# A two-layer encoder trunk: the order of every engine's instructions taken from the scheduler's other machine model

## The chip, the cores and the metric

The kernel runs on one core of a Trainium2 chip. A core has five engines that each work through an instruction list of their own, in the order in which it was written: TensorE (in the profile PE, its weight loads PEld), VectorE (DVE), ScalarE (ACT), GpSimd (POOL) and SyncE (SP), which here issues nearly all DMA transfers. They meet only at semaphores: an instruction that has to wait for another engine holds up everything behind it on its own list.

The metric is the device time of one execution in microseconds (us). Lower is better.

## The reference

One sequence of 1024 tokens of width 1024 goes through two layers. Layer 0 mixes tokens with multi-head latent attention (8 heads, a low-rank query and key/value, a rotary part, a mask by chunks of 64). Layer 1 mixes them with an mLSTM, a matrix memory that is carried from chunk to chunk. After each follows a gated MLP of width 2816 with a causal width-3 convolution. Every sub-layer is normalised, and shifted, scaled and gated by a vector that is computed from the conditioning `c`.

```python
for i in range(2):
    mod = silu(c) @ mod_w[i] + mod_b[i]
    sh_a, sc_a, g_a, sh_f, sc_f, g_f = split(mod, 6)
    h = rms_norm(x) * (1 + sc_a) + sh_a
    y = mla_mixer(h, ...) if i == 0 else mlstm_mixer(h, ...)
    x = x + g_a * y
    h = rms_norm(x) * (1 + sc_f) + sh_f
    a, g = split(h @ w_up, 2)
    a = causal_conv3(a, conv_w, conv_b)
    x = x + g_f * ((gelu(a) * g) @ w_down)
return rms_norm(x, final_norm)
```

All inputs and outputs are float32.

## The kernel before

**Precision and units of work.** Every float32 operand of a large matrix product is split into a rounded part (`whi`, `h` and so on, written by ACT) and the rest (`wlo`, written by DVE or POOL). One product of two tiles is then three TensorE instructions, the lines 175, 176 and 177 of the function `mm3`; each streams 512 columns as a rule. A weight tile comes by a DMA on SP's queue (`wraw`, `raw`, `mraw`), ACT casts it (line 167 or 988), DVE subtracts (168 or 989), and TensorE uses it.

**Stages.** They follow each other in the program text with some overlap: the input projection of both token halves (tiles `ia`); the attention, 16 turns of one head and one token half, in which the score blocks (`sc`, line 673), the turning of the weights (`pT`, 696), the product with the values (`pv`) and the projections of the next head (`qp`, `kp`, `qrp`, `vp`) are woven into each other by a written list of steps; the output projection (`op`); the MLP, in which each 2x2 block of products is done with 7 instead of 8 products, first the upward part (`pa`, `pb`, `pd`), then the downward part (`da`, `db`), whose operands `U` are rebuilt on ACT and DVE from `u` read back from DRAM; the mLSTM, whose matrix `C` is a serial chain of 7 links for each of 4 heads (lines 1471 to 1476) and is covered by projections (`inp`) placed between the links; and again an output projection and an MLP. The conditioning is not a matrix product: a row of 1024 numbers is multiplied and summed on DVE in one instruction (`mod_dot`, line 198), 96 of these rows in all, spread over the stages.

**What sets the order.** The function `trunk_kernel` is traced once, as plain Python; each call appends an instruction. The tile framework notes what depends on what. When the `with` block closes, its scheduler runs the program on a model of the machine. Whenever an engine of the model is free, it gets that instruction among those whose inputs and buffers are ready in the model which has the highest priority. Priority is the place in the program text, raised inside `tc.high_priority()`. `tc.keep_in_program_order` ties an instruction behind the one that was traced before it on its engine. The order that comes out is fixed for each engine, the semaphore waits are put in afterwards, and on the chip each engine follows its list whatever the real durations are. So the model has a say wherever it takes an instruction for not yet ready: what is behind it in the text then goes ahead of it.

How far that goes can be counted in the built program, the scheduled list of each engine against the traced one. Of TensorE's 10,421 matrix instructions 89% stand at their place in the text, and in both MLPs' upward parts nearly all. On DVE 11% do, and one is moved by 6.5 places on average; on ACT 16% and 3.6 places; on SP's queue of 746 transfers 14% and 7.3 places.

**Lookahead.** In the MLPs the weights of a product are made several products before it is run (`LOOK = (7, 5)`: for the first products the product and the seven behind it, later the product and the five behind it); they lie in four buffers of two halves each (`open_weights(4, 2)`), and raw tiles in `RAWS = 5`. In the attention two turned tiles are made ahead (`TURN = 2`). PSUM has four `mm` tiles, and four of another kind that depends on the stage.

The two places of the code that the steps of the prediction come back to are the chain of the mLSTM and the row product:

```python
with tc.high_priority():
    dve.scalar_tensor_tensor(Cn, C, gcl(GDEC, hd, cc), pc, ALU.mult, ALU.add)   # 1473 (1471 at the first link)
    C = Cn
    act.activation(Cs[0], C, AF.Copy)                                           # 1475
    dve.tensor_tensor(Cs[1], C, Cs[0].bitcast(F32), ALU.subtract)               # 1476
...
tc.keep_in_program_order(mod_dot(l, j * 8 + k, raw, c))                         # 198, in mod_steps
```

The function that the change touches:

## Time and profile before

| | |
|---|---|
| Median of 3 runs | 2197.2 us (2195.38 to 2199.59) |
| Span of the profiled execution | 2200.1 us; no other time is given for it |
| TensorE busy | 2166.5 us, 98% of the span |
| TensorE weight loads (beside the matmuls) | 1818.0 us, 83% |
| VectorE busy | 1693.1 us, 77% |
| ScalarE busy | 1046.7 us, 48% |
| GpSimd busy | 178.3 us, 8% |
| Mean granted TensorE clock | 0.994 of full speed |
| DMA | 270.50 MB, mean 123 GB/s |

Busy time is the share of the span in which the engine had an instruction in work. TensorE's instructions overlap: each is recorded with a duration of some 0.39 us while one starts every 0.23 us, so the share says how seldom TensorE stood still, not how fast it went. The profiled execution lies 2.9 us above the median of the runs; a difference that is worked out in the trace is therefore taken over to the median as it is.

### The profile page before, as it was taken

Reading aid. Unit: us, or ns where it says so; the run is one execution under the profiler, and the core shown is the slowest. Engines: PE = TensorE matmul, PEld = TensorE weight load, DVE = VectorE, ACT = ScalarE, POOL = GpSimd, SP = SyncE. Lnnn points to the kernel's source line nnn. Section 1 sums busy time; section 2 is a strip of 40 time slices with the busy share of each in tenths; the row PEclk is TensorE's granted clock in tenths of the full one; section 3 lists DMA queues with packets and bytes.
Section 4 is the critical chain, followed back from the end, with each engine's and each line's share of the span. In section 5 each row is a group of like instructions: output and inputs, shape, how many; then the busy total and the mean of one; then the engine's idle time right before and its main releaser. Section 6 shows DMA issues by size and latency. Waiting matters only on the chain.

```text
span 2200.1 us, 28740 instructions
## 1 busy us (share of the span) xinstructions
PE 2166.5 (98%) x10557; PEld 1818.0 (83%) x10557; DVE 1693.1 (77%) x2769; ACT 1046.7 (48%) x1812; POOL 178.3 (8%) x216
## 2 busy tenths in 40 slices
PE   9999999999999999999999999999999999999998
PEld 7878888787888888877888888988788888887787
DVE  8877878669878777899973655566887777778997
ACT  6465556446544444543453434344554444453335
POOL 0000000000000000042210111010000000002232
PEclk9999999999999999999999999999999999999999
DMA  8512234832444332542132243444143332245122
GB/s 317 152 50 63 92 109 142 285 125 69 157 139 143 123 125 85 204 151 89 53 121 93 62 131 103 132 157 171 64 144 101 111 120 92 79 163 194 50 80 77
DMA packets 105085, 270.50 MB, mean 123 GB/s; under 512 B 12336, under 2 KB 15984, under 8 KB 104944
## 3 DMA queue, kind: packets, MB, share of 16 engines
q1 hardware_dynamic: 104544, 268.28, 36.9%
q8 instruction: 83, 1.36, 0.3%
q14 instruction: 58, 0.48, 0.1%
q10 hardware_dynamic: 400, 0.39, 0.1%
HBM read 221.53 MB, written 44.47 MB: 121 GB/s over the span
## 4 chain that ended last, share of the span: by engine, by line
PE 85%; DVE 9%; DMA 3%; ACT 2%; issue 1%; POOL 0%; SPq 0%; POOLq 0%; DVEq 0%; ACTq 0%
PE pa L175 7%; PE pa L177 7%; PE pa L176 7%; PE pd L177 3%; PE pd L175 3%; PE pd L176 3%; PE sc L673 3%; PE op L175 3%; PE op L176 3%; PE op L177 2%; PE inp L177 2%; PE da L175 2%; PE inp L175 2%; PE inp L176 2%; PE da L176 2%; PE db L175 2%
## 5 line engine op out<-in xcount | busy, mean ns | idle before, releaser
L988 ACT ACTIVATE whi<-raw 128x512 fp32r<-128x512 f32 (+1 forms) x252 | 147.3, 607 | 243.2 <-PE pb L176 61.0
L988 ACT ACTIVATE whi<-wsum 128x512 fp32r<-128x512 f32 (+1 forms) x224 | 134.0, 617 | 181.8 <-PE pa L176 61.5
L175 PE MATMUL pa<-T,whi 128*128 128x512 f32 x528 | 205.9, 390 | 0.0
L176 PE MATMUL pa<-T,whi 128*128 128x512 f32 x528 | 205.4, 389 | 0.0
L177 PE MATMUL pa<-T,wlo 128*128 128x512 f32 x528 | 205.1, 389 | 0.0
L989 DVE TENSOR_TENSOR wlo<-wsum,whi 128x512 fp32r<-128x512 f32 (+1 forms) x224 | 151.1, 690 | 32.8 <-ACT whi L988 31.5
L989 POOL TENSOR_TENSOR wlo<-raw,whi 128x512 fp32r<-128x512 f32 (+1 forms) x80 | 119.9, 1515 | 401.7 <-ACT whi L988 394.0
L175 PE MATMUL da<-U,whi 128*128 128x512 f32 (+1 forms) x364 | 139.5, 383 | 3.4 <-DVE x L294 3.4
L177 PE MATMUL da<-U,wlo 128*128 128x512 f32 (+1 forms) x364 | 138.4, 383 | 2.0 <-DVE wlo L989 2.0
L176 PE MATMUL da<-U,whi 128*128 128x512 f32 (+1 forms) x364 | 139.2, 382 | 0.0
L989 DVE TENSOR_TENSOR wlo<-raw,whi 128x512 fp32r<-128x512 f32 (+1 forms) x172 | 115.7, 679 | 24.9 <-ACT whi L988 24.9
L167 ACT ACTIVATE whi<-wraw 128x1024 fp32r<-128x1024 f32 x67 | 70.7, 1059 | 117.1 <-PE op L176 59.2
L175 PEld LDWEIGHTS pa<-T,whi 128*128 128x128 f32 x528 | 99.1, 188 | 22.2 <-ACT whi L988 1.2
L177 PEld LDWEIGHTS pa<-T,wlo 128*128 128x128 f32 x528 | 99.1, 188 | 20.6
L176 PEld LDWEIGHTS pa<-T,whi 128*128 128x128 f32 x528 | 99.1, 188 | 20.3
L1140 DVE TENSOR_TENSOR U<-q,U 128x1024 fp32r<-128x1024 f32 x84 | 102.9, 1241 | 14.0 <-ACT U L1139 13.6
L1028 ACT ACTIVATE ct<-a,cols 128x512 f32<-128x512 f32 x88 | 70.8, 808 | 83.9 <-DVE a L1050 47.9
L175 PE MATMUL db<-U,whi 128*128 128x512 f32 x264 | 103.3, 391 | 1.3 <-ACT whi L988 1.3
L168 DVE TENSOR_TENSOR wlo<-wraw,whi 128x1024 fp32r<-128x1024 f32 x67 | 81.7, 1222 | 29.4 <-ACT whi L167 27.2
L177 PE MATMUL db<-U,wlo 128*128 128x512 f32 x264 | 102.9, 390 | 0.0
L176 PE MATMUL db<-U,whi 128*128 128x512 f32 x264 | 102.8, 389 | 0.0
L1139 ACT ACTIVATE U<-q 128x1024 fp32r<-128x1024 f32 x84 | 79.7, 979 | 47.7 <-DVE q L1138 22.2
(378 smaller groups left out, 6097.3 us busy)
## 6 DMA issues: line engine op xcount, KB each, us to landing
raw<-in_wf SPq DMA_DIRECT2D x96, 512.0 KB, 4.0
wraw<-in_w SPq DMA_DIRECT2D x67, 512.0 KB, 3.7
mraw<-in_mod_w SPq DMA_DIRECT2D x56, 512.0 KB, 4.0
ud<-ct SPq DMA_DIRECT2D x88, 256.0 KB, 2.4
q<-ud SPq DMA_DIRECT2D x88, 256.0 KB, 4.6
raw<-in_wd SPq DMA_DIRECT2D x32, 512.0 KB, 6.4
pa<-in_mod_w SPq DMA_DIRECT2D x24, 512.0 KB, 3.7
x<-xd SPq DMA_DIRECT2D x48, 256.0 KB, 4.8
```

The lines of the kernel that those rows point to most:

```text
L167: act.activation(hi, raw, AF.Copy)
L168: dve.tensor_tensor(lo, raw, hi.bitcast(F32), ALU.subtract)
L175: pe.matmul(ps, lh, rh, start=first, stop=False, skip_group_check=more)
L176: pe.matmul(ps[:, 0:rl.shape[-1]], lh, rl, start=False, stop=False, skip_group_check=more)
L177: pe.matmul(ps, ll, rh, start=False, stop=last, skip_group_check=more)
L673: pe.matmul(ps[:, cs], a[:, qs if n < 3 else qrs_], b[:, cs], start=n == 0, stop=n == 4)
L988: act.activation(hi, src, AF.Copy)
L989: eng.tensor_tensor(lo, src, hi.bitcast(F32), ALU.subtract)
L1028: act.activation(t, a[:, 2:], AF.Identity, bias=col(f"cb{l}", m), scale=cw(m, 2))
L1139: act.activation(hi, w, AF.Copy)
L1140: dve.tensor_tensor(lo, w, hi.bitcast(F32), ALU.subtract)
```

## The change

The flag `schedule_with_timeline_sim` of the tile framework is set. The scheduler then runs the program on its other machine model (a simulator of timelines, in which each instruction holds devices for stretches of time) instead of the default one. The traced program, its dependencies, its priorities, the tiles, their buffers and the computation are the same; the order on each engine, and with it the places of the semaphore waits, is what the scheduler makes of the other model's times.

```diff
-    with tile.TileContext(nc) as tc:
+    with tile.TileContext(nc, schedule_with_timeline_sim=True) as tc:
         trunk_kernel(tc, *args)
```

## The prediction

> **What bounds the kernel now.** I read the page's busy shares and the clock first, then the busy time by stages, then who TensorE waited for, and last the order of the instructions around single waits.
>
> ```profile
> span 2200.1 us, 28740 instructions
> PE 2166.5 (98%) x10557; PEld 1818.0 (83%) x10557; DVE 1693.1 (77%) x2769; ACT 1046.7 (48%) x1812; POOL 178.3 (8%) x216
> ...
> core 0: 2200.1 us, clock 0.994
> ```
>
> TensorE stood still for 2200.1 - 2166.5 = 33.6 us. The mean clock of 0.994 is 0.006 x 2200.1 = 13 us of lost full speed more. The same 10,557 matmuls run in any order, so an order can win at most 33.6 + 13 = 47 us; it can lose without a bound that this page shows. Where the 33.6 us lie is told by the windows (length, then busy time and number of instructions of PE, PEld, DVE, ACT and POOL, clock, DMA):
>
> ```profile
> 0.00:110.00 110.00, 105.22 (x504) 87.99 (x505) 91.57 (x162) 57.51 (x89) 7.63 (x14) 0.97 0.68 234
> 110.00:400.00 290.00, 284.14 (x1585) 243.88 (x1583) 228.18 (x488) 171.91 (x352) 5.50 (x30) 0.99 0.32 99
> ...
> 535.00:930.00 395.00, 395.00 (x1743) 326.40 (x1742) 318.65 (x508) 183.13 (x299) 1.79 (x18) 1.00 0.43 143
> 930.00:1110.00 180.00, 177.01 (x777) 145.14 (x776) 166.71 (x210) 72.41 (x115) 58.65 (x40) 1.00 0.28 95
> 1110.00:1500.00 390.00, 384.99 (x2256) 337.51 (x2255) 227.11 (x470) 165.33 (x332) 34.95 (x40) 1.00 0.38 123
> ...
> 1595.00:1990.00 395.00, 395.00 (x1742) 326.42 (x1741) 302.41 (x474) 182.84 (x299) 1.79 (x18) 1.00 0.37 122
> 1990.00:2145.00 155.00, 151.30 (x662) 123.42 (x661) 145.30 (x184) 59.07 (x90) 46.91 (x28) 1.00 0.28 92
> 2145.00:2200.10 55.10, 46.53 (x257) 40.14 (x255) 40.68 (x65) 31.03 (x65) 16.37 (x15) 0.92 0.22 77
> ```
>
> The two upward parts of the MLPs, 790 us, have no idle time at all and full clock: 395.00 / 1743 = 0.2266 us from one matmul to the next. The idle time is 4.8 us at the start, 5.9 in the attention, 3.0 and 3.7 in the downward parts, 5.0 in the mLSTM, 8.6 in the last stage, and 2.7 in the stretches not shown. Start and end wait for first loads and for the last norm, which every order has: about 13 us that I count as fixed. The movable rest is some 20 us, plus the clock.
>
> What TensorE waited for (total, times, longest):
>
> ```profile
> PE da L175 <- DVE x L294: 3.4, 5, 1.0
> ...
> PE po L176 <- DVE C L1476: 2.1, 2, 1.2
> PE da L177 <- DVE wlo L989: 2.0, 2, 1.0
> PE kp L175 <- ACT ckvn L495: 1.9, 1, 1.9
> ...
> PE pv L175 <- DVE pl L605: 1.3, 4, 0.3
> ...
> PE po L175 <- ACT C L1475: 0.7, 2, 0.5
> ```
>
> No engine is the bound here. These are serial links of the program (a product's rest `wlo`, the matrix `C`, a turned tile) that came late by 0.3 to 1.9 us.
>
> **The change, part by part.** Nothing is added or removed. What moves is which instruction of DVE, ACT and SP stands before which, and TensorE's own order where the text leaves a choice. I price four places.
>
> *The upward parts.* Here another order on DVE, ACT and SP costs nothing as long as a product's weights are early enough, and they are: the weights are made five products ahead, a product is 12 matmuls, so the lead is 5 x 12 x 0.2266 = 13.6 us.
>
> ```profile
> 642.47 0.39 PE L175 MATMUL pa<-T,whi 128*128 128x512 f32 x1
> ...
> 642.49 0.63 ACT L988 ACTIVATE whi<-raw 128x512 fp32r<-128x512 f32 x1 [0.70 <-PE pa L176]
> ```
>
> The cast started as soon as a product had ended that held its buffer: ACT is ahead as far as buffers let it, and waits. SP is held up most by the stores of `u`, which wait for DVE, with the loads of raw weights behind them:
>
> ```profile
> SPq L1036 <- DVE ct L1035: 427.9, 83, 11.5
> ```
>
> The longest of these, 11.5 us, is under 13.6 us. So I put 0 for both upward parts. If the order moved such a store ahead by one more product (2.7 us), 11.5 + 2.7 = 14.2 us would exceed the lead by 0.6 us: from 0 to about 0.6 us for a step that has it; 0 is nearer, since 83 stores wait on average 427.9 / 83 = 5.2 us.
>
> *One link in detail.* The wait of 1.24 us in the mLSTM shows what an order does:
>
> ```profile
> 1343.99 0.42 DVE L1471 COPY C<-pc 128x258 f32<-128x258 f32 x1
> ...
> 1344.45 0.42 ACT L1475 ACTIVATE C<-C 128x258 fp32r<-128x258 f32 x1 [0.77 <-DVE C L1471]
> ...
> 1344.92 1.22 DVE L198 SCALAR_TENSOR_TENSOR mraw<-mraw,crow 128x1024 f32<-128x1024 f32 x1
> ...
> 1346.06 0.43 DVE L1476 TENSOR_TENSOR C<-C,C 128x258 fp32r<-128x258 f32 x1
> ...
> 1346.55 0.39 PE L176 MATMUL po<-C,qw 128*128 128x258 f32 x1 [1.24 <-DVE C L1476]
> ```
>
> ACT's copy of `C` ended at 1344.45 + 0.42 = 1344.87, DVE came free at 1344.92, but a row product of 1.22 us was next on its list: in the model the copy was not yet ready at that point. The rest of `C` came 1.2 us late and TensorE stood. Where the other model ends ACT's copy slightly sooner, the two change places and the wait is gone; where it ends another copy later, a wait like this appears at another link. That is the change's price and its gain, a piece of DVE's list of about 1.2 us at a time.
>
> *The clock behind a wait.*
>
> ```profile
> 1344.50:1347.90 3.40, 1.74 (x9) 1.45 (x10) 3.40 (x7) 1.53 (x6) 0.00 (x0) 1.00 0.66 190
> 1347.90:1351.30 3.40, 3.40 (x9) 2.65 (x9) 2.52 (x5) 1.13 (x3) 0.63 (x1) 0.50 0.80 265
> ...
> 115.60:122.50 6.90, 5.85 (x16) 4.86 (x17) 5.08 (x13) 4.79 (x10) 0.00 (x0) 0.51 0.41 114
> 949.00:954.40 5.40, 4.39 (x19) 3.30 (x18) 5.40 (x6) 1.53 (x2) 2.19 (x2) 1.00 0.94 317
> ```
>
> After 3.4 us in which TensorE was busy for 1.74 us, the clock was 0.50 for the next 3.4 us, which costs 1.7 us. After idle time of 5.40 - 4.39 = 1.0 us in 5.4 us it stayed at 1.00. So two waits close together cost about 1.7 us on top of their own length, single ones nothing. The Trainium skill, page "TensorE: Matmul & The Clock Gate", section "HAM oscillation — how this bites in real kernels", gives as the rule "no PE-idle gaps >~3.4µs". By that rule no wait of this size would touch the clock, and the sum below would be 3.4 us smaller, 2207 us; the trace disagrees, since its longest gap here was 1.24 us.
>
> *The sum.* Links at which an order can put something in between: 28 of the mLSTM's chain (4 heads x 7), 64 score blocks (16 turns x 4), 42 operands of the downward parts (2 x 21): 134. The waits quoted above that belong to these (da 5 and 2, po 2 and 2, pv 4) are 15 in 134, 11%, with 3.4 + 2.0 + 2.1 + 0.7 + 1.3 = 9.5 us. The bounds: none of them left, -9.5 us; all 134 late by the mean of 9.5 / 15 = 0.63 us, +75 us. DVE is busy 227.11 of 390 us in the mLSTM, 228.18 of 290 in the attention and 166.71 of 180 in the first downward part, so a link that comes free finds DVE in work in 58 to 93% of cases, whatever stands there; that only 11% come late belongs to this particular list. I take a share twice as large, 22%: nearer the low bound, because the other list also follows the text's priorities, above chance because many more links run without a wait now than with one, so that a shift has more to lose than to win. That is +9.5 us for the waits and +3.4 us for two more drops of the clock, 12.9 us: 2197.2 + 12.9 = 2210 us against the median, 2213 us for a span like the profiled one.
>
> **The rivals.**
>
> *Faster: the joint at 111 to 122 us closes.* TensorE waits there for the normalised key/value input:
>
> ```profile
> 111.98 0.69 DVE L478 TENSOR_TENSOR pa<-pa,cs 128x512 f32<-128x512 f32 x1
> ...
> 112.58 0.69 DVE L479 TENSOR_TENSOR pa<-pa,cs 128x512 f32<-128x512 f32 x1
> ...
> 112.88 0.50 PE L175 MATMUL qrp<-cqn,whi 128*128 128x512 f32 x1 [0.59 <-ACT cqn L495]
> ...
> 113.85 0.69 DVE L480 TENSOR_TENSOR pa<-pa 128x512 f32<-128x512 f32 x1
> 113.99 0.50 PE L176 MATMUL qrp<-cqn,whi 128*128 128x512 f32 x1 [0.61 <-DVE cqn L496]
> ...
> 114.45 1.41 DVE L494 SCALAR_TENSOR_TENSOR raw<-raw,inb,pa 128x512 f32<-128x512 f32 x2
> ...
> 115.88 1.34 ACT L495 ACTIVATE ckvn<-raw,cols 128x512 fp32r<-128x512 f32 x2
> ...
> 116.65 0.79 PE L175 MATMUL kp<-ckvn,whi 128*128 128x512 f32 x1 [1.93 <-ACT ckvn L495]
> ```
>
> Three rotary instructions (lines 478 to 480, 3 x 0.69 = 2.07 us) stand on DVE ahead of line 494, whose result `kp` needs. Behind it they would cost nothing here, and the wait of 1.93 us would go; with the two of 0.59 and 0.61 us, 3.1 us of idle time and the half clock of 6.9 us after them (3.4 us) are at stake: 6.5 us. The link at 1344 adds 1.24 + 1.7 = 2.9 us. Both right and nothing lost elsewhere is -9.4 us, 2188 us. For it speaks that these are plain errors of the present model. Against it, it decides only if fewer than about seven of the 134 links become late at 0.63 us and 1.7 us of clock for every second or third. Chance 0.24.
>
> *No change.* The two lists may differ where nobody waits, or hardly differ; the upward parts and the projections, which wait for nothing, are over half of the span. 2197 us. Chance 0.17.
>
> *Much slower: the cover of the chains is used up early.* If the other model lets TensorE take the projections placed between the mLSTM's links before the links are ready, each link stands bare: 0.42 + 0.42 + 0.43 = 1.27 us, with the clock 1.7 us. Half of the 28 links bare give 14 x 2.97 = 42 us, 2239 us; all of them 83 us, 2280 us. Against it: in the text TensorE has at most a few tiles to run ahead into. For it: 11% of TensorE's instructions already stand elsewhere than in the text (the count in the section on the kernel). Chance 0.14.
>
> **How the numbers follow.** My forecast, a few more late links, has 0.45, and by itself 2202 to 2229 us: from half of the added waits without the clock, 9.5 / 2 = 4.8 us, to a share of late links four times the present one, 3 x 9.5 = 28.5 us, with the same 3.4 us of clock. The faster case goes from 2183 to 2193 us, the large one from 2229 to 2280 us. A range of 2186 to 2250 us leaves out about 0.08 below and 0.07 above. About 0.2%, 4.4 us, is what a measurement of this kernel can tell from no change. Faster 0.24, same 0.17, slower 0.45 + 0.14 = 0.59.
>
> **What the profile after would show.** The upward parts again with no idle time and 0.2266 us per matmul; if they have idle time, the lead of 13.6 us was not enough and the first step is wrong. The waits of TensorE on `C`, `pl`, `wlo` and `x` 25 to 35 in number instead of 15 and 15 to 20 us instead of 9.5; if they are as before and the time is longer, the loss is in DMA or in a stage boundary that I put at nothing. A clock below 0.994 with some two more half-speed stretches. Line 478 to 480 before or after 494 decides the first rival; bare links in the mLSTM, with a row of waits of about 1.3 us on line 1475 or 1476, the third. The prediction is wrong if the new list puts the first loads or the last norm differently, which I count as fixed, or if TensorE's own list changes in the MLPs.

## The result and the profile after

| | before | after |
|---|---|---|
| Median of the runs beside each other | 2196.65 us (2195.38 to 2199.59) | 2259.51 us (2257.12 to 2261.84) |
| Ratio, 95% interval | | 1.0283 (1.0269 to 1.0296) |
| Span of the profiled execution | 2200.1 us | 2260.1 us |
| TensorE's list: instructions that left their place in the text; mean shift | 11%; 0.95 places | 50%; 10.1 places |
| DVE's list | 89%; 6.5 | 92%; 8.0 |
| ACT's list | 84%; 3.6 | 92%; 4.6 |
| SP's list | 86%; 7.3 | 88%; 8.1 |

The kernel became 62.9 us slower. The lower half of the table is counted as in the section on the kernel. VectorE, ScalarE and SyncE had left the text already and leave it a little further. The new thing is TensorE's list: the other model lets TensorE run ahead of the text, most of all in the mLSTM (60% of its instructions there, by 26 places on average).

The head of the page of after, and its line of the clock from the view of the cores:

```profile
span 2260.1 us, 28726 instructions
...
PE 2180.5 (96%) x10557; PEld 1832.7 (81%) x10557; DVE 1690.6 (75%) x2769; ACT 1040.8 (46%) x1812; POOL 184.1 (8%) x216
```

```profile
core 0: 2260.1 us, clock 0.982
```

The same 10,557 matmuls. TensorE stood still for 2260.1 - 2180.5 = 79.6 us instead of 33.6, which is 46.0 more, and was busy for 14.0 us longer with the same matmuls, at a lower mean clock: 0.982 instead of 0.994. The two add up to the 60.0 us between the spans. Where it stood, by the windows of after (columns as in the prediction):

```profile
545.00:925.00 380.00, 380.00 (x1678) 314.67 (x1677) 301.42 (x485) 176.73 (x291) 1.79 (x18) 1.00 0.39 124
1622.00:2005.00 383.00, 383.00 (x1690) 316.79 (x1690) 287.46 (x454) 177.51 (x292) 1.78 (x18) 1.00 0.31 101
925.00:975.00 50.00, 40.55 (x169) 32.62 (x168) 42.20 (x54) 17.68 (x24) 0.00 (x0) 0.90 0.68 231
2005.00:2055.00 50.00, 40.49 (x169) 32.58 (x168) 42.15 (x55) 17.00 (x23) 0.00 (x0) 0.90 0.66 226
85.00:125.00 40.00, 31.30 (x157) 26.44 (x157) 29.64 (x48) 19.36 (x30) 4.85 (x4) 0.83 0.20 64
400.00:425.00 25.00, 19.79 (x91) 16.07 (x90) 15.15 (x28) 7.80 (x14) 0.00 (x0) 0.86 0.64 202
525.00:545.00 20.00, 15.27 (x56) 11.75 (x56) 20.00 (x25) 14.59 (x21) 0.00 (x0) 0.83 0.16 53
1150.00:1200.00 50.00, 44.50 (x200) 35.81 (x199) 34.34 (x52) 22.68 (x32) 2.82 (x5) 0.93 0.31 100
```

The first two rows are the upward parts: full, as before. The other six are the joints between stages: from the upward to the downward part (twice), the input norms, the end of the attention, the norm ahead of the first upward part, and the entry of the mLSTM. In 235 us they hold 9.5 + 9.5 + 8.7 + 5.2 + 4.7 + 5.5 = 43.1 of the 79.6 us, and the clock is down in each. The waits of TensorE in after (total, times, longest) name the same places:

```profile
PE db L175 <- ACT whi L988: 18.8, 2, 9.5
PE pd L176 <- DVE T L918: 8.8, 2, 4.4
PE da L175 <- DVE x L294: 6.9, 4, 2.7
PE op L175 <- ACT oh L727: 5.2, 1, 5.2
PE rb L262 <- DVE raw L494: 5.1, 2, 2.9
...
PE pv L176 <- DVE pl L605: 3.3, 6, 1.8
...
PE pc L175 <- DVE C L1471: 0.5, 1, 0.5
```

Few waits, and long ones. No `po` waits for `C` any more, and one `pc` waits for 0.5 us: in the mLSTM the links are covered.

A ledger shows the same by stage. Each matmul is given the median time from one start to the next of its shape; for all of them that is 2136 us in both kernels. How far the real starts lag behind this sum, after minus before, grows by 7.5 us over the input norms and the first turns, 9.0 over the attention, 5.5 at the first `op`, 5.5 from there into the first upward part, 9.3 at the first joint of upward and downward part, 1.9 in the first downward part, 7.8 at the entry of the mLSTM, by -8.0 in the rest of the mLSTM and its output projection, 6.5 at the second start of an upward part, 9.5 at the second joint, and 5.6 from there to the end: 60.1 us in all.

**The costliest joint, line by line.** The order of TensorE's products at the end of the upward part, by the number of matmuls in a row:

```
before  903.6: da 4, pa 12, da 20, pa 12, da 24, db 132 ...
after   930.9: da 28, pa 12, da 8, db 28, pa 12, db 20, da 12, (idle) db 64 ...
```

In after, `da` and `db` of the downward part run ahead of the last two `pa` of the upward part, whose operands, by the rule of the scheduler, were not yet ready in the other model. The last `pa` start at 937.3 and 948.2 us instead of 904.6 and 912.0, so that the last `ct` (line 1035) ends 24.7 us after the first `da` instead of 12.2. SP's queue of after:

```profile
952.65 0.36 SPq L1036 DMA_DIRECT2D ud<-ct  x1
953.05 2.50 SPq L1222 DMA_DIRECT2D x<-xd  x5
955.70 0.34 SPq L1036 DMA_DIRECT2D ud<-ct  x1
959.14 0.80 SPq L1121 DMA_DIRECT2D q<-ud  x2
960.03 1.81 SPq L1152 DMA_DIRECT2D raw<-in_wd  x4
```

and of before:

```profile
915.85 0.33 SPq L1036 DMA_DIRECT2D ud<-ct  x1
916.22 4.22 SPq L1222 DMA_DIRECT2D x<-xd  x6
920.53 2.79 SPq L1152 DMA_DIRECT2D raw<-in_wd  x4
947.19 3.65 SPq L1121 DMA_DIRECT2D q<-ud  x8
```

The raw weights of `db` (line 1152) wait for nothing here, but they stand behind transfers that do. What the queue itself waited for (total, times, longest), in after from 930 to 962 us and in before from 900 to 925 us:

```profile
SPq L1222 <- PE pa L177: 14.7, 2, 7.5
```

```profile
SPq L1036 <- DVE ct L1035: 5.5, 2, 3.9
SPq L1222 <- PE pa L177: 4.2, 2, 2.9
```

The loads of `x` (line 1222) wait for the last two `pa`, and in after these come late; the last stores of `ct` follow at once behind them, then two loads of `q` (3.0 us more of waiting), then the weights. They leave at 960.03. What follows in after, by the timeline:

```profile
966.61 0.69 DVE L1163 TENSOR_TENSOR wsum<-raw 128x512 f32<-128x512 f32 x1 [3.69 <-DMA raw<-in_wd]
967.40 0.63 ACT L988 ACTIVATE whi<-wsum 128x512 fp32r<-128x512 f32 x1 [6.58 <-DVE wsum L1163]
...
968.08 0.79 PE L175 MATMUL db<-U,whi 128*128 128x512 f32 x1 [9.30 <-ACT whi L988]
...
968.67 0.63 PE L176 MATMUL db<-U,whi 128*128 128x512 f32 x1
...
969.10 0.63 PE L177 MATMUL db<-U,wlo 128*128 128x512 f32 x1
```

TensorE used up the work that had covered these loads, stood for 9.30 us, and began again at half clock: a matmul every 0.43 us. The cause is TensorE's order, through the queue: it makes the last `pa` late, and the weights stand behind what waits for them. SP's own order adds nothing against before at this point: from the last store to the weights it is 4.3 us in after and 4.7 us in before, where loads of `x` stood in between.

### The profile page after: what moved, and what is told of

The parts are those of the page before. It is cut to its first block, busy times and chain, and to the rows that moved or that the text cites. A ratio compares the mean times of both kernels' runs of the same rounds, so it can differ in the third digit from the quotient of the medians.

```text
span 2260.1 us, 28726 instructions
## 1 busy us (share of the span) xinstructions
PE 2180.5 (96%) x10557; PEld 1832.7 (81%) x10557; DVE 1690.6 (75%) x2769; ACT 1040.8 (46%) x1812; POOL 184.1 (8%) x216
## 4 chain that ended last, share of the span: by engine, by line
PE 86%; DVE 7%; DMA 3%; ACT 2%; issue 1%; SPq 1%; POOL 0%; DVEq 0%; POOLq 0%; ACTq 0%
PE pa L175 7%; PE pa L176 7%; PE pa L177 7%; PE pd L176 4%; PE pd L177 4%; PE pd L175 4%; PE da L175 3%; PE da L176 3%; PE da L177 3%; PE inp L176 3%; PE inp L177 3%; PE inp L175 3%; PE db L175 3%; PE sc L673 3%; PE db L176 2%; PE db L177 2%
## 5 line engine op out<-in xcount | busy, mean ns | idle before, releaser
L989 DVE TENSOR_TENSOR wlo<-wsum,whi 128x512 fp32r<-128x512 f32 (+1 forms) x224 | 145.9, 676 | 13.2 <-ACT whi L988 12.9
L175 PE MATMUL db<-U,whi 128*128 128x512 f32 x264 | 105.1, 398 | 18.8 <-ACT whi L988 18.8
L175 PE MATMUL inp<-h,whi 128*128 128x512 f32 x256 | 101.7, 400 | 3.7 <-DVE x L294 2.1
L175 PE MATMUL op<-oh,whi 128*128 128x512 f32 x256 | 100.0, 393 | 5.2 <-ACT oh L727 5.2
```

Of the source, the lines that this page charges most:

```text
L175: pe.matmul(ps, lh, rh, start=first, stop=False, skip_group_check=more)
L989: eng.tensor_tensor(lo, src, hi.bitcast(F32), ALU.subtract)
```

## The experiments

A list is carried from one kernel to the other in this way: the program is built once on the other model, and while it is built again a dependency that only fixes the order of issue, without a semaphore, is laid from each instruction of an engine to the next one of the foreign list. In the second form (shortened below) only instructions whose place in the traced text (15,800 instructions) lies in a window are tied.

```diff
+    for engines, lo, hi in PIN:
+        for e in engines:
+            order = [n for n in other if engine[n] == e and lo <= place[n] < hi]
+            for a, b in zip(order, order[1:]):
+                tc.add_manual_dep(text[place[b]], a, NoSync, reason="pin")
```

`a_` is the changed kernel with lists of the one before; `b_` is the kernel before with lists of the changed one. Work, tiles and buffers are the same in all of them. A kernel that is built with its own lists tied in this way has every instruction at the same place as without, so the ties by themselves change no list. But a list that is left free is not kept as it was: the model makes it anew around the tied ones. In a_va, TensorE's free list has 42% of its instructions at their place in the list of before and 46% at their place in that of after; in a_pe, DVE's has 47% and 52%. Each was timed beside runs of the kernel before on the same chip, with medians of 2196.1 to 2197.2 us; a cost below is the difference of the medians.

### Whole lists of single engines

The first theories were: A, late joints, made by SP's queue and TensorE's list; B, many small late links on DVE and ACT.

```diff
+FLAG, PIN = True, ("SP",)                            # a_sp
+FLAG, PIN = True, ("PE",)                            # a_pe
+FLAG, PIN = True, ("DVE", "Activation", "Pool")      # a_va
+FLAG, PIN = True, ("PE", "SP")                       # a_pesp
```

a_sp, SyncE's queue from before:

> The changed kernel (other model) with one edge more per transfer, so that SP's queue runs in the order that it has in the kernel before; all other engines are ordered by the other model. Theory A (two causes: SP's queue with loads stuck behind a transfer that waits, and TensorE's norm joints placed late): the waits db<-whi (9.5 us twice, with the half clock behind them) and op<-oh (5.2 us) go, the waits on T line 918 (4.4 us twice) stay: about 28 us less than the changed kernel, 2231 us. Theory B (mine from the prediction, many small late links on DVE and ACT): SP is no cause, 2255 to 2262 us.

2278.18 us, ratio 1.0372 (1.0357 to 1.0387).

a_pe, TensorE's list from before:

> The changed kernel with TensorE's list pinned to the order of the kernel before, all other engines by the other model. Theory A: the late joints (rb of the second half 8 us of matmul work later in both output projections, 7.5 us at the input norms, 7.8 us at the entry of the mLSTM) go, about 29 us less, and the 8 us that the other model won in the mLSTM's chain may go too: 2231 to 2240 us; the waits of 9.5 us stay. Theory B: TensorE's list is no cause, 2255 to 2262 us.

2288.68 us, 1.0418 (1.0403 to 1.0434).

a_va, the lists of VectorE, ScalarE and GpSimd from before:

> The changed kernel with the lists of DVE, ACT and GpSimd pinned to those of the kernel before, TensorE and SP by the other model. Theory A: these lists are no cause of their own; what SP and TensorE lose stays: 2240 to 2262 us. Theory B: nearly all of the 62 us comes back: 2197 to 2210 us.

2302.49 us, 1.0489 (1.0474 to 1.0505).

a_pesp, TensorE's list and SyncE's queue from before:

> The changed kernel with TensorE's and SP's lists both pinned to those of the kernel before, DVE, ACT and GpSimd by the other model. Theory A: the two add up, nearly all of the 62 us comes back: 2197 to 2210 us. Theory B: the loss stays, 2250 us or more.

2306.77 us, 1.051 (1.0492 to 1.0527).

All four are slower than the changed kernel, 2259.5 us. Neither A nor B stands in the form in which I had put it: taking back one engine's list, or these two or three, does not take back the loss. With TensorE's old list the waits on the late weights go and others of the same kind come, by the waits of a_pe:

```profile
PE st L250 <- DVE ssq L241: 9.8, 2, 8.5
PE da L175 <- DVE ct L1035: 7.5, 2, 3.8
```

DVE's list in a_pe is neither that of before nor that of after, and why it makes these operands late was not followed further. A whole list mixes many joints, so the next runs went by place.

### By place: the joints and the mLSTM

Theory C: TensorE's list is the root, and carried over alone it carries the loss.

```diff
+FLAG, PIN = True, ((("PE",), 6530, 6930), (("PE",), 14096, 14496),)      # a_joint
+FLAG, PIN = False, ((("PE",), 6530, 6930), (("PE",), 14096, 14496),)     # b_joint
+FLAG, PIN = True, ((("PE",), 3317, 4313), (("PE",), 10864, 11913),)      # a_norm
+FLAG, PIN = False, ((ALL, 8363, 10833),)                                 # b_ml
```

a_joint, TensorE's old order at both joints of upward and downward part:

> The changed kernel, with only TensorE's list pinned to that of the kernel before, and only around the two joints from the upward to the downward part of the MLPs (the last 6 upward products and the first 12 downward ones, 400 instructions of the text each); everything else by the other model. Theory C (TensorE's list is the root: it runs the downward products B11 and B21 ahead of the last products pa<-T, so the last stores of u, and behind them on SP the loads of x and of the weights, come late): the two waits db<-whi of 9.5 us shrink to 1 us or less, with lag of TensorE 9.4 us less at each joint: about 2259 - 19 = 2240 us. Theory D (SP's and DVE's lists put the loads late by themselves): the waits stay, 2255 to 2262 us.

2254.25 us, 1.0264 (1.0249 to 1.028): 57.1 us instead of 62.9, so 5.8 of the 18.8 us that these joints have in the ledger. `db <- whi` is gone, and two waits `da <- ct` (line 1035) with 7.5 us in all came in its place. DVE's list in these windows has 22% of its instructions at their place in before and 34% at that in after; that it makes `ct` late by what it puts ahead of it was not shown.

b_joint, TensorE's new order at these joints in the kernel before:

> The kernel before (default model), with only TensorE's list at the same two joints pinned to that of the changed kernel. Theory C: the waits db<-whi appear, about 2197 + 19 = 2216 us. Theory D: 2195 to 2202 us.

2209.57 us, 1.0057 (1.0042 to 1.0072): 12.4 us. The order of products is that of after (da 28, pa 12, da 8, db 28 and so on), and the same wait is there, by its waits:

```profile
PE db L175 <- ACT whi L988: 11.6, 2, 5.8
```

SP's queue of b_joint is the default model's answer to that order:

```profile
924.31 0.32 SPq L1036 DMA_DIRECT2D ud<-ct  x1
924.68 2.82 SPq L1222 DMA_DIRECT2D x<-xd  x6
927.60 2.03 SPq L1152 DMA_DIRECT2D raw<-in_wd  x4
```

The loads stand in the same row as before, behind the last store and the loads of `x` but ahead of those of `q`; 927.60 instead of 920.53 us. What held the queue is the same as in after, by its waits from 900 to 932 us:

```profile
SPq L1222 <- PE pa L177: 12.5, 2, 7.6
```

So TensorE's order, with what the default model makes of the other lists around it, is enough for this loss. The wait at the first joint is 5.79 us here and 9.30 in after. Of these 3.5 us, 2.1 come from the last `ct`, which ends 22.6 us after the first `da` instead of 24.7, and 1.0 from the place of the weights, 3.3 us behind the last store instead of 4.3.

a_norm, TensorE's old order from the output projection to the first products of the upward part:

> The changed kernel, with only TensorE's list pinned to that of the kernel before from the start of each output projection to the 24th upward product behind it; everything else by the other model. Theory C: the rows of the norm (rb) come 8 us of matmul work earlier, the two waits pd<-T line 918 of 4.4 us go, 5.5 us at each place: about 2248 us. Theory D: T is late because DVE's list is, the waits stay, 2257 to 2262 us.

2260.27 us, 1.0286 (1.0271 to 1.0302): no gain. The waits of `pd` on `T` (4.4 us each) are gone, and others came: `pa <- g` (line 1076) twice, 4.8 us in all. In the ledger the place itself gains 6.7 us and what follows loses 4.6.

b_ml, all five lists of the changed kernel in the mLSTM:

> The kernel before (default model), with the lists of all five engines pinned to those of the changed kernel in the mLSTM alone (from the first value projection to the output projection), where TensorE's lag grew by 8 us less in the changed kernel. If the gain belongs to these lists: 2189 us, faster than both. If it was only the slack that the changed kernel had bought with 7.8 us more of waiting at the entry of this stage: 2195 to 2205 us.

2191.55 us, 0.9971 (0.996 to 0.9983): faster than both kernels. The changed kernel's order is better there.

### All joints, and the text in place of a list

After a_joint and a_norm, C alone was not enough. Theory E: the lists fit only lists of the same model, and the loss is the sum over the joints at which all lists of the changed kernel meet. In b_ml, b_p1 and b_p2 all five are tied, so that in their windows the order is exactly that of the changed kernel.

```diff
+FLAG, PIN = False, ((ALL, 0, 1000), (ALL, 3317, 4700), (ALL, 7950, 8363), (ALL, 10864, 12300),)   # b_p1
+FLAG, PIN = False, ((ALL, 1000, 3317), (ALL, 6400, 7300), (ALL, 13970, 14870),)                   # b_p2
+FLAG, PIN = False, ((("PE",), 8363, 10833),)                                                      # b_mlpe
```

b_p1, all lists in the input, around both starts of an upward part, and at the entry of the mLSTM:

> The kernel before, with the lists of all five engines pinned to those of the changed kernel in four windows of the text: the input projection with its norms, the two stretches from an output projection to the first upward products, and the entry of the mLSTM. Theory E (each engine's list only fits the other lists of the same model, and the loss is a sum over these joints): TensorE's lag grows by the ledger's 7.5, 5.5, 7.8 and 6 us at these places, 2197 + 27 = 2224 us. Theory F (the loss at a place comes from what an earlier place did to the lists, so that a transplanted joint costs little): under 2208 us.

2224.47 us, 1.0127 (1.0113 to 1.0141): 28.0 us.

b_p2, all lists in the attention and at both joints of upward and downward part:

> The kernel before, with the lists of all five engines pinned to those of the changed kernel in the attention with the first output tiles and at the two joints from the upward to the downward part. Theory E: 5 us in the attention, 8.8 us at its end, 11 and 12 us at the joints, 2197 + 37 = 2234 us, with the waits db<-whi of about 9.5 us and op<-oh of about 5 us. Theory F: under 2212 us.

2227.18 us, 1.0142 (1.0128 to 1.0156): 30.7 us. The two kernels share out the waits of after between them. First b_p1, then b_p2:

```profile
PE pd L176 <- DVE T L918: 8.8, 2, 4.4
PE rb L262 <- DVE raw L494: 5.1, 2, 2.9
```

```profile
PE db L175 <- ACT whi L988: 17.1, 2, 9.3
PE op L175 <- ACT oh L727: 5.2, 1, 5.2
```

With b_ml's -5.6 us the three sets give 28.0 + 30.7 - 5.6 = 53.1 of the 62.9 us. The rest is some 10 us. The ledger has 1.9 + 5.6 = 7.5 us in the downward parts and at the end, which no run carried over; whether the rest lies there, or the three sets do not quite add up, no run tells, since none holds all of them.

b_mlpe, TensorE's list alone in the mLSTM:

> The kernel before, with TensorE's list alone pinned to that of the changed kernel in the mLSTM. If TensorE taking the covering projections ahead of po<-C is what wins there: as with all five lists, 2189 to 2193 us and no wait on C. If the other engines' lists win (row products behind the links on DVE): 2196 to 2205 us.

2188.29 us, 0.9964 (0.9952 to 0.9976): the fastest kernel of all. Here C holds: TensorE's list, with what the default model makes of the others around it, brings the whole gain. The windows of the mLSTM, before and then b_mlpe:

```profile
1150.00:1460.00 310.00, 305.82 (x1894) 272.94 (x1893) 167.56 (x386) 129.95 (x283) 29.50 (x34) 0.99 0.31 101
```

```profile
1150.00:1460.00 310.00, 308.75 (x1927) 277.32 (x1926) 176.45 (x401) 130.76 (x288) 27.25 (x34) 1.00 0.33 107
```

Idle time 1.25 us instead of 4.18, full clock, and 33 matmuls more in the same 310 us. The timeline of b_mlpe at the link that the prediction shows for before (1343.99 to 1346.55 us there):

```profile
1336.40 0.42 DVE L1471 COPY C<-pc 128x258 f32<-128x258 f32 x1
...
1337.59 0.42 DVE L1476 TENSOR_TENSOR C<-C,C 128x258 fp32r<-128x258 f32 x1
...
1342.05 0.28 PE L175 MATMUL po<-C,qw 128*128 128x258 f32 x1
```

Between the link's `pc` and `po <- C` TensorE runs 30 projection matmuls (`inp`) instead of 12. The rest of `C` is there 4 us before it is used; in before it was 1.24 us late.

b_text, the kernel before with this written into the text (default model): a link's product with the matrix moved behind the next piece of cover.

```diff
-                if cc > 0:
-                    mm3(po, [x[:, cs] for x in qw], Cs, False, True)
+                Cp = Cs if cc > 0 else None
 ...
+                yield
+                if cc > 0:
+                    mm3(po, [x[:, cs] for x in qw], Cp, False, True)
 ...
-                yield
```

> The kernel before on the default model, with the mLSTM's text changed so that the product po<-C of a link stands behind the next piece of the cover instead of ahead of it, using the matrix C of the link before; nothing else. If the gain in the mLSTM is that TensorE gives the link more time: 2189 to 2193 us, faster than both, no wait of po on C in the trace. If the gain depends on the other lists of the changed kernel: 2196 to 2200 us.

2191.3 us, 0.9979 (0.9969 to 0.9988): 5 of b_mlpe's 8 us, with no foreign list. The waits on `C` are gone.

### TensorE's list against the other four, and the best of both

```diff
+FLAG, PIN = False, ((("PE",), 0, 1000), (("PE",), 1000, 3317), ... the seven windows of b_p1 and b_p2)   # b_wpe
+FLAG, PIN = False, ((REST, 0, 1000), (REST, 1000, 3317), ... the same; REST is SP, DVE, ACT, POOL)       # b_wrest
```

b_wpe, TensorE's list alone in the seven windows:

> The kernel before, with TensorE's list alone pinned to that of the changed kernel in all seven windows of the two transplants before (input, attention, both stretches behind an output projection, both joints in the MLPs, entry of the mLSTM). All five lists in these windows cost 28.0 + 30.7 = 59 us. If TensorE's list is the root everywhere (theory C): 2197 + 50 or more = 2246 us or more. If it is half of it, as at the joints of the MLPs (12.4 of about 24 us): about 2225 us. If the other lists are the cause: under 2210 us.

2278.16 us, 1.037 (1.0356 to 1.0385): 82.0 us.

b_wrest, the other four lists there, TensorE's left to the default model:

> The same seven windows, with the lists of SP, DVE, ACT and GpSimd pinned to those of the changed kernel and TensorE's left to the default model. Theory C: the default model keeps TensorE near the text, and little is lost: 2200 to 2212 us. If each list only fits the others of its model (theory E): as much as with all five or more, 2245 us or more.

2314.39 us, 1.0535 (1.052 to 1.0549): 118.3 us.

All five lists in the same windows cost 28.0 + 30.7 = 58.7 us in two kernels. Either half without the other costs more than both together. By the ledger 53 of the 118 us of b_wrest arise in the attention, where all five lists (b_p2) cost 5.5. This is what E had said for the windows taken together; at the two joints of upward and downward part alone, TensorE's list cost 12.4 us in b_joint, less than the 18.8 us of the ledger. And it holds for a tied list with whatever the model then makes of the free ones: in b_wpe DVE's list has 32% of its instructions in these windows at their place in before and 41% at that in after. What TensorE's new list would cost with the old lists of the others, unchanged, was not run. Why TensorE's list alone does well in the mLSTM and badly over these windows is not shown either.

b_best, b_text and the reorder that the prediction's first rival was about (line 494 ahead of lines 478 to 480):

```diff
-            norm_gain(raw[:, 4:6], inb[:, 4:6], rb, 2, "kvn", ...)
+            with tc.high_priority(): norm_gain(raw[:, 4:6], inb[:, 4:6], rb, 2, "kvn", ...)
```

> The kernel before on the default model with two changes of its text: the mLSTM's po<-C behind the next piece of the cover (2191.3 us by itself), and the norm of the key/value input raised to high priority, which puts line 494 ahead of the rotary lines 478 to 480 on DVE at the joint at 111 us. By the price of the prediction's first rival the second is worth up to 6.5 us: 2185 to 2189 us, no wait of kp on ckvn. If the joint is limited by something else there: 2190 to 2193 us.

2191.67 us, 0.9974 (0.9965 to 0.9984): by the medians no more than b_text. Its nine runs lie from 2187.8 to 2192.8 us, so that a gain of 2 or 3 us would not be seen; the profiled one, with 2188.5 us, is at the low end. The window around the joint, before and then b_best, and a wait that b_best has and before has not:

```profile
90.00:140.00 50.00, 46.58 (x236) 39.00 (x235) 43.00 (x82) 31.43 (x57) 2.39 (x4) 0.93 0.24 70
```

```profile
90.00:140.00 50.00, 45.76 (x244) 38.01 (x244) 43.10 (x85) 30.73 (x56) 2.39 (x4) 1.00 0.25 73
```

```profile
PE qp L175 <- DVE v L605: 2.2, 1, 2.2
```

The wait of `kp` (1.9 us) is gone and the clock is full. But the rotary instructions now stand ahead of the rest of `v` (line 605), and TensorE waits there: 0.82 us more idle time, not less. The 8 matmuls more that this execution has in the window go with its full clock.

## Why the prediction was right or wrong

**The direction** was right, and the size wrong: 12.9 us forecast, 62.9 measured.

**The upward parts** were right: 380.00 / 1678 = 0.2265 us per matmul, no idle time. TensorE's own list did change there (35% of the instructions from place 4700 to 6400 of the text left theirs, by 3.5 places on average) and it cost nothing: that change was no sign of a loss by itself.

**No large bound**: right. No engine became the limit; DVE is busy for 1690.6 us instead of 1693.1.

**The sum** is the step that failed. It priced the change as more late links of 0.63 us on DVE, from a share of 11% to 22%. The waits of that kind (`da` on `x` and `wlo`, `po` on `C`, `pv` on `pl`) are 10 in number with 6.9 + 3.3 = 10.2 us, against 15 with 9.5 before: the term that was to double did not move, where 25 to 35 waits were forecast. The loss was in the stage joints, for which the sum had no term. The prediction had said that then "the loss is in DMA or in a stage boundary that I put at nothing"; b_p1 and b_p2 show it, with 58.7 us.

**Why there was no such term.** The 134 links were counted on DVE, and TensorE's list was taken for nearly the text's, as it was before. It left it in half of its places. At a joint work of two stages can be ready, and at the costliest one the work that ran ahead delayed the joint's own last products, and with them the loads that the next products needed. That the other joints lose in the same way is likely from their waits, but was not followed line by line. The step priced SP's queue too (11.5 us of waiting ahead of a store against a lead of 13.6 us), but only inside the upward part, where it is harmless. At its end the queue stood for 14.7 us on the last `pa`, instead of 4.2, and TensorE for 9.3.

**The clock** was under-priced by the same step. Two more half-clock stretches at 1.7 us were put in; TensorE's busy time grew by 14.0 us, with 13 stretches at half clock instead of 4. That waits of this size bring half clock with them was right, and the trace of after has a stretch that shows it without a gap of 3 us, in the input norms:

```profile
95.00:98.00 3.00, 0.96 (x7) 0.58 (x5) 2.01 (x4) 1.23 (x2) 1.01 (x1) 1.00 0.00 0
98.00:101.00 3.00, 1.09 (x4) 0.72 (x4) 3.00 (x6) 1.47 (x3) 0.00 (x0) 0.57 0.00 0
101.00:104.00 3.00, 1.08 (x4) 0.71 (x4) 3.00 (x6) 1.98 (x3) 0.00 (x0) 0.50 0.00 0
```

That single waits cost nothing was wrong. One wait of 1.76 us in the attention (`pv` on `pl`, 389.87 to 391.63 us) was followed by 3.4 us at half clock:

```profile
388.60:392.00 3.40, 1.64 (x10) 1.11 (x9) 3.38 (x8) 1.36 (x4) 0.00 (x0) 1.00 0.80 219
392.00:395.40 3.40, 3.40 (x15) 3.08 (x14) 3.37 (x8) 1.52 (x4) 0.41 (x2) 0.50 0.92 339
```

The longest wait in the input norms is 2.9 us (`rb` on line 494, above). The rule "no PE-idle gaps >~3.4µs" (the Trainium skill, page "TensorE: Matmul & The Clock Gate", section "HAM oscillation — how this bites in real kernels") agrees with what follows the waits of 9.3, 5.2 and 4.4 us, a clock of 0.50 each time, and would have had full clock in both of these stretches; the trace shows 0.50.

**The first rival** was wrong in sign for after and in price in general. The changed kernel lost 7.5 us in the ledger where it was to win 6.5, and b_best, which makes the edit that the rival described, shows no gain by the medians and more idle time in the window: "Behind it they would cost nothing here" overlooked line 605. The half clock did go in the profiled execution of b_best.

**The third rival** saw that TensorE might run ahead in the mLSTM, and put a loss of 42 to 83 us on it. TensorE did run ahead, into `inp`, and it gained: it took the cover before it took the link's product, which gave the chain more time and not less. That the rival's stretch of 2229 to 2280 us holds the measured time is chance.

**What stays open.** Some 10 of the 62.9 us were not carried over by any run. Why the other model takes the last operands of a stage for late, so that TensorE runs ahead there, was not tried. Nor was the direct remedy at the costliest joint, the loads of the weights moved ahead of those of `x` on SP's queue.

## What to carry to other kernels

When only the order changes, look first at where TensorE's own list will leave the text, and then at the joints between stages. How far it leaves does not tell the sign: it was moved most in the mLSTM, which won, and in the upward parts it was moved at no cost. The costliest place here was one where loads that wait for nothing stand in a queue behind loads that wait for the last products of a stage. Take the orders of several engines over by stage with all lists together; over the seven windows here, lists that were carried without the others cost more than the whole. Where a stage does win, the order that wins can be written into the text: here one product moved behind the next piece of cover, 5 of the 8 us.

## What the runs showed that was not expected

The lists of one model fit each other to a degree that I had not expected: in the same windows five lists cost 58.7 us, TensorE's with the rest made anew around it 82.0, and the other four with TensorE's made anew 118.3 us.

Short waits can bring half clock as a long one does: with waits of 2.91 and 2.22 us, TensorE was busy for about 1 us of every 3, and the clock stood at 0.50 to 0.57 in 98 to 104 us of after. A single wait of 1.76 us was enough for 3.4 us at 0.50.
